# A conditional overflow path moved from the end of each mixture of experts to behind its first four experts, and five modulation chunks moved with it

## The chip, the cores and the metric

The kernel runs on one core of a Trainium2 chip, as one program. The metric is the device time of one execution in microseconds (us); lower is better. Several engines work side by side in a core: TensorE (PE, matrix multiplications; PEld is its loading of weights into the array), VectorE (DVE), ScalarE (ACT), GpSimd (POOL) and SyncE (SP), which here does nothing but issue transfers from the chip's memory (DMAs). Each engine executes its own instructions in order, and waits at semaphores for the others.

## What is computed

Two layers of a backbone over 256 latent tokens and 256 context tokens of width 1024. Each layer has three token mixers on one input projection, and then a mixture of experts. Cut to what matters here:

```python
for l in range(2):
    mod = silu(c) @ w_mod[l] + b_mod[l]          # modulation: 6 vectors of 1024
    h = modulate(rms_norm(x, g_norm[l, 0]), sh1, sc1)
    x = x + gt1 * token_mixers(h, ...)           # starts with h @ w_in[l]
    h = modulate(rms_norm(x, g_norm[l, 1]), sh2, sc2)
    x = x + gt2 * hier_moe(h, ...)               # 32 experts, top 2 for each token
# an expert: (silu(h @ w_gate) * (h @ w_up)) @ w_down, times the router's weight
```

Layer 0 treats all 512 tokens. Layer 1 needs only the latent ones in its experts, 256 tokens.

## The kernel before, in words

`mixers(l)` and `moe(l)` run for l = 0 and then l = 1. A tiling framework puts the instructions of each engine in an order of its own, by estimated due times. It does not move instructions across a conditional block (`tc.If`); between two such blocks it mixes pieces of the program that the code writes one after the other.

**The experts.** `moe` takes the 32 experts in eight groups of four (q = 0 to 7). For each group, `gather` (L1237) picks the tokens of its experts by matrix multiplications with one-hot matrices (`one_hots`, L1226), up to 32 tokens for each expert; `gate_up` (L1274) multiplies them with eight slabs of weights of 1 MB; `swiglu` (L1281 to L1284) works on ACT and DVE; `act_T` (L1294) transposes its result on PE; `down` (L1309) multiplies with four more slabs; and `combine` (L1203 on PE, L1208 on DVE) adds the result to the residual `xT` (tiles called qkv in the traces). `scatter_mats` (L1256, L1259) builds the matrices for `combine`. In layer 0 all this is done for two halves of the tokens (`ns` = 2), in layer 1 for one.

**The slabs.** The weights come through a ring of slots: seven in layer 0; sixteen in layer 1, of which two are used only once. `fetch_up` and `fetch_down` issue the transfers on SP (L1010), in the order of use, and each waits until PE has used up the slab that stood in its slot. In layer 1 the sixteen slabs of q = 0 and q = 1 are fetched ahead of the experts.

**The overflow path.** An expert may be chosen by more than 32 tokens. Then the slots do not do, and a dense path treats the tokens that are left. All of it stands in a block `tc.If(top >= 1024 + CAP)` at the end of `moe`. The highest rank is loaded from memory into a register of each engine (L1359, an instruction TENSOR_LOAD), and each engine branches over the block if there is no overflow (L1361, COMPARE_AND_BRANCH). In the run shown there is none in either layer. The body is 162 rows of PE's order in layer 0 and 103 in layer 1; 125 and 89 on DVE; 30 on SP.

**The layer boundary.** At the end of layer 0's `moe` stand, in the code: the last `combine`; the split of the weights for layer 1's first projection into two parts (`prep`, L221 and L222); five modulation chunks (`mod_chunk`: a fetch of 1 MB at L1355, sixteen multiplications at L238, a copy at L241, two transposes at L243, and L246 and L247 on DVE); the conditional block; the spill of `xT` to memory (L1430). Then `mixers(1)` begins. Its first projection (`pre_w`, L333 to L335: three products for each pair of tiles, 48 in all) works on `xT` times a scale (`scaled`, L369 on ACT and L370 on DVE, sixteen each), before the norm is known. `shift_share` (L399) computes what the shift adds. The norm takes the sums of squares (`Stats`, L276), a column sum on PE (L285), L289 on DVE, a power on POOL (L292), and a broadcast on PE and ACT (L300, L304). Then `shifted` (L322, L327, L329, L378, L379) forms the normalised input h that all further projections use.

## Time and profile before

| | us |
|---|---|
| runs of the kernel before | 1631.34, 1634.6, 1635.05 |
| median | 1634.6 |
| the profiled execution | 1629.37 |
| its span (first to last instruction) | 1627.5 |
| experts of layer 0, from the first gather to the last combine | 709.4 to 970.7 |
| from there to the end of the second projection of layer 1 | 970.7 to 1021.3 |
| experts of layer 1, from the first gather to the last residual | 1407.0 to 1622.4 |

The profile is of one execution. All times below are on its axis; us from the span's start. [...] A line of waits names the instruction that stood, and the one that let it go. "PEq" and "PEldq" are PE's own sequencer, "SPq" is SP's.

### The profile page before, as it was taken

The page shows a single profiled execution, that of the slowest core. Times are in us where ns is not written, and L with a number is a line of the kernel's source. Part 1 is how long each engine was busy: PE and PEld are TensorE (multiplying, and loading weights), DVE is VectorE, ACT ScalarE, POOL GpSimd, SP SyncE. Part 2 cuts the span into 40 slices and gives each one's busy share as a digit, 9 for nine tenths or more (in the row PEclk, how much of TensorE's full clock was granted, in tenths as well). Part 3 has the DMA queues.
Part 4 walks back from the last instruction along what each step waited for, and adds up shares of the span by engine and source line. Part 5 has one row for each costly group of instructions (what it writes and reads, how often), then busy time and mean ns, then how long its engine had stood idle before and what let it go on. Part 6 is the DMA issues. An engine that isn't in the chain of part 4 may idle for free. (4 is left out here: it accounts for less than half of the span.)

```text
span 1627.5 us, 26096 instructions
## 1 busy us (share of the span) xinstructions
PE 1529.6 (94%) x10725; PEld 1058.8 (65%) x10725; DVE 788.3 (48%) x1774; ACT 571.8 (35%) x1125; POOL 183.2 (11%) x162
## 2 busy tenths in 40 slices
PE   5999999999999999989999997999999999897875
PEld 3688789767767778844434435989978789632221
DVE  4637943443345425363333457378456556441222
ACT  4425642443344333131211135356355444211100
POOL 2200320100011003010000003003101112100000
PEclk9999999999999999989999998999999999898888
DMA  8552334323322154349999994542225448699998
GB/s 303 194 172 79 108 107 156 117 76 115 127 98 84 40 179 149 121 166 382 375 398 413 377 409 185 209 142 74 91 104 175 169 148 325 231 411 416 417 418 325
DMA packets 57199, 349.26 MB, mean 215 GB/s; under 512 B 6912, under 2 KB 8032, under 8 KB 20336
## 3 DMA queue, kind: packets, MB, share of 16 engines
q1 hardware_dynamic: 54720, 341.02, 54.9%
q10 hardware_dynamic: 1616, 5.24, 0.9%
q0 software_dynamic: 736, 1.24, 0.4%
q8 instruction: 88, 1.44, 0.4%
q14 instruction: 39, 0.32, 0.1%
HBM read 344.33 MB, written 3.15 MB: 213 GB/s over the span
## 5 line engine op out<-in xcount | busy, mean ns | idle before, releaser
L222 DVE TENSOR_TENSOR wlo<-wraw,whi 128x1024 fp32r<-128x1024 f32 (+1 forms) x152 | 190.6, 1254 | 169.3 <-ACT whi L221 154.2
L333 PE MATMUL mm<-h,whi 128*128 128x512 f32 (+1 forms) x656 | 226.9, 348 | 0.0
L334 PE MATMUL mm<-h,whi 128*128 128x512 f32 (+1 forms) x656 | 223.4, 342 | 0.0
L335 PE MATMUL mm<-h,wlo 128*128 128x512 f32 (+1 forms) x656 | 222.2, 342 | 0.0
L221 ACT CAST whi<-wraw 128x1024 fp32r<-128x1024 f32 (+1 forms) x152 | 155.6, 1026 | 172.3 <-PE mm L334 68.7
L333 PE MATMUL mm<-whi,h 128*128 128x256 f32 (+1 forms) x640 | 183.1, 289 | 0.0
L335 PE MATMUL mm<-whi,h 128*128 128x256 f32 (+1 forms) x640 | 182.9, 288 | 0.0
L334 PE MATMUL mm<-wlo,h 128*128 128x256 f32 (+1 forms) x640 | 182.3, 286 | 0.0
L333 PEld LDWEIGHTS mm<-h,whi 128*128 128x128 f32 x656 | 123.8, 189 | 35.5 <-issue 17.9
L335 PEld LDWEIGHTS mm<-h,wlo 128*128 128x128 f32 x656 | 123.5, 189 | 22.6 <-issue 10.1
L334 PEld LDWEIGHTS mm<-h,whi 128*128 128x128 f32 x656 | 124.2, 190 | 16.9 <-issue 5.3
L333 PEld LDWEIGHTS mm<-whi,h 128*128 128x128 f32 x640 | 121.5, 191 | 6.6 <-issue 4.0
L334 PEld LDWEIGHTS mm<-wlo,h 128*128 128x128 f32 x640 | 122.2, 191 | 1.0 <-DVE G L763 0.5
L335 PEld LDWEIGHTS mm<-whi,h 128*128 128x128 f32 x640 | 121.7, 191 | 1.5 <-issue 1.4
L1274 PE MATMUL at<-qkv,y 128*32 128x512 f32 x792 | 101.2, 606 | 8.0 <-DMA qkv<-in_wgu 8.0
L1208 DVE SCALAR_TENSOR_TENSOR qkv<-mm,c_modT,qkv 128x256 f32<-128x256 f32 x192 | 80.2, 477 | 34.6 <-PE mm L1203 34.6
L618 DVE TENSOR_REDUCE nmx<-at 128x1 f32<-128x512 f32 (+1 forms) x96 | 56.7, 598 | 54.7 <-PE at L604 53.9
L1274 PE MATMUL at<-wraw,y 128*32 128x512 f32 x552 | 73.7, 634 | 7.8 <-DMA wraw<-in_wgu 7.8
L1282 DVE SCALAR_TENSOR_TENSOR a<-a,at 128x256 f32<-128x256 f32 x24 | 10.1, 420 | 141.0 <-ACT a L1281 141.0
L536 POOL TENSOR_TENSOR s1p<-s1p,c_powm 128x8 f32<-128x8 f32 (+1 forms) x24 | 43.3, 1806 | 302.4 <-DVE s1p L534 101.1
L620 ACT ACTIVATE a<-at,nmx 128x512 f32<-128x512 f32 (+1 forms) x96 | 59.3, 619 | 34.3 <-DVE nmx L618 34.1
L1281 ACT ACTIVATE a<-at 128x256 f32<-128x256 f32 x24 | 9.2, 383 | 176.4 <-PE at L1274 171.3
(373 smaller groups left out, 2579.1 us busy)
## 6 DMA issues: line engine op xcount, KB each, us to landing
qkv<-in_wgu SPq DMA_DIRECT2D x62, 1024.0 KB, 11.6
wraw<-in_win SPq DMA_DIRECT2D x56, 1024.0 KB, 4.9
wraw<-in_wgu SPq DMA_DIRECT2D x42, 1024.0 KB, 11.4
wraw<-in_wmod SPq DMA_DIRECT2D x39, 1024.0 KB, 5.0
qkv<-in_wdn SPq DMA_DIRECT2D x31, 1024.0 KB, 9.6
wraw<-in_wdn SPq DMA_DIRECT2D x19, 1024.0 KB, 10.9
h<-in_wgu SPq DMA_DIRECT2D x14, 1024.0 KB, 17.6
wraw<-in_wbr SPq DMA_DIRECT2D x24, 512.0 KB, 3.4
```

What stands on the lines that cost most here:

```text
L221: nc.scalar.copy(hv, src)
L222: nc.vector.tensor_sub(lv, src, hv.bitcast(F32))
L333: nc.tensor.matmul(out_, lhsT=lh, rhs=rh, start=first, stop=False)
L334: nc.tensor.matmul(out_, lhsT=lh, rhs=rl, start=False, stop=False)
L335: nc.tensor.matmul(out_, lhsT=ll, rhs=rh, start=False, stop=last)
L536: nc.gpsimd.tensor_tensor(out=r, in0=v, in1=powm[:, :2 * H], op=ALU.pow)
L618: nc.vector.tensor_reduce(nmx[:, hf:hf + 1], S[hf], axis=AX.X, op=ALU.max, negate=True)
L620: nc.scalar.activation(P[hf], S[hf], AF.Exp, bias=nmx[:, hf:hf + 1], scale=1.0, accum_out=sm[:, hf:hf + 1])
L1208: nc.vector.scalar_tensor_tensor(xT[f][:, c], p[:, c], modT[l][:, 40 + f, v_:v_ + 1], xT[f][:, c], op0=ALU.mult, op1=ALU.add)
L1274: nc.tensor.matmul(gps[v_][CAP * e:CAP * e + CAP], lhsT=xe[v_][:, k, s0:s0 + CAP], rhs=w[e], start=(k == 0), stop=(k == KT - 1))
L1281: nc.scalar.activation(th[:, 0:256], gp[:, 0:256], AF.Tanh, bias=0.0, scale=0.5)
L1282: nc.vector.scalar_tensor_tensor(th[:, 0:256], th[:, 0:256], 1.0, gp[:, 0:256], op0=ALU.add, op1=ALU.mult)
```

## The change

Three things are done.

- **The block moves.** It becomes the function `overflow`, called once in each `moe` after everything that the code writes for q = 0: the first `gate_up`, `swiglu`, the fetches, `scatter_mats(1)`, the gathers and `act_T(0)`. Its body is rewritten to need only small tiles: it loads 512 columns of weights at a time into working tiles (`a2`) and transposes the tokens anew for each expert, since at this place the large slots hold weights that are in use. The body is 662 rows of PE's order in layer 0 and 334 in layer 1; 313 and 169 on DVE; 390 and 198 on SP.
- **The fetches.** `fetch_up` and `fetch_down` put their wishes in a list (`pending`); `pump` issues them as slots come free, and `give_back` returns a slot as soon as a slab is used. The order of the transfers and the number of slots stay.
- **The modulation chunks.** The five chunks leave the end of `moe`. In `mixers(1)`, three are fetched into tiles `y` ahead of the first projection and computed behind it, and two more follow by `mod_fill(2)`.

The diff, cut to its core; the body of the block keeps its arithmetic.

```diff
--- before.py
+++ after.py
@@ -699,9 +699,19 @@
+        held = []
+        if l == 1:
+            for tag in ("y", "y", "y"):
+                m, w = mods.pop(0), s8(tag, [KT, 256])
+                nc.sync.dma_start(w, T["wmod"][m])
+                held.append((m, w))
         for c in range(2):
             if c < len(pre_w):
                 proj_f(pre_w[c], N, lambda i, p: use_k(2 * c + i, p, True), h0, l0)
+                for m, w in held:
+                    mod_chunk(*m, pat, w)
+                mod_fill(2 if held else 0)
+                held = []
...
-            slot_tags[:] = ["qkv"] * 4 + ["mg", "y"] + ["qkv"] + ["h"] * 2 + ["wraw"] * 2 + ["mg", "wraw"] + ["whi", "wlo"] * 3
+            slot_tags[:] = ["qkv"] * 4 + ["mg", "y"] + ["qkv"] + ["h"] * 2 + ["wraw"] * 2 + ["mg", "wraw"] + ["whi"] * 3
...
+    def pump():
+
+        while pending and slot_tags:
+            key, src = pending.pop(0)
+            fetched[key] = fetch_slot(slot_tags.pop(0), src)
+
+    def take(key):
+        return fetched[key][1]
+
+    def give_back(key):
+        tag = fetched.pop(key)[0]
+        if tag not in ("mg", "y"):
+            slot_tags.append(tag)
+        pump()
...
-            fetched.setdefault(("up", q), []).extend(fetch_slot(T["wgu"][l, q, k]) for k in ks)
+            pending.extend((("up", q, k), T["wgu"][l, q, k]) for k in ks)
+            pump()
...
-                w = fetched["up", q][k]
+                w = take(("up", q, k))
...
+                give_back(("up", q, k))
...
+        def overflow():
+
+            top = nc.values_load(mi[0:1, 0:1], min_val=0, max_val=2048,
+                                 skip_runtime_bounds_check_because="the key is 1024 + a rank below 512, or a rank")
+            with tc.If(top >= 1024 + CAP):
...
+                def weights(src):
+                    w = a2([512])
+                    nc.sync.dma_start(w, src.rearrange("o p n -> p (o n)"))
+                    return w
+
+                with tc.For_i(0, NQ, 1) as q4:
+                    one = bass.ds(q4, 1)
+                    for e in range(4):
...
+                        for t in range(ntt):
+                            gp = pat()
+                            for k in range(KT):
+                                q = ptr()
+                                c = slice(128 * k, 128 * k + 128)
+                                for part, ht in enumerate((hth, htl)):
+                                    nc.tensor.matmul(
+                                        q[:, :128], lhsT=ht[t // 2][:, t % 2, c].bitcast(F32), rhs=ident,
+                                        start=(part == 0), stop=(part == 1))
+                                hk = a2([512])[:, :128]
+                                nc.vector.tensor_copy(hk, q[:, :128])
+                                nc.tensor.matmul(
+                                    gp, lhsT=hk, rhs=weights(T["wgu"][l, one, k, :, e]), start=(k == 0), stop=(k == KT - 1))
...
-                aT = act_T(q - 1)
+                if q > 1:
+                    aT = act_T(q - 1)
...
+            if q == 0:
+                aT = act_T(0)
+                overflow()
         down(NQ - 1, act_T(NQ - 1))
         combine(NQ - 1)
         if l == 0:
             lead.append((prep(T["win"][1, 12]), norm_scale(1, 0, slice(0, KT))))
-            for _ in range(5):
-                w = s8("qkv", [KT, 256])
-                nc.sync.dma_start(w, T["wmod"][mods[0]])
-                mod_chunk(*mods.pop(0), pat, w)
-
...
-        top = nc.values_load(mi[0:1, 0:1], min_val=0, max_val=2048,
-                             skip_runtime_bounds_check_because="the key is 1024 + a rank below 512, or a rank")
-        with tc.If(top >= 1024 + CAP):
...
-            if nxt[0] is not None:
-                nxt[0].n = 0
-                for f in range(KT):
-                    nxt[0].step(xT[f])
-            else:
-                for f in range(0, KT, 2):
-                    emit(f)
         return nxt[0]
```

**TensorE in layer 0, around the first four experts.** Before, the last gathers for q = 2 and 3 are followed by the transposes of q = 0 (L1294, `tr`) and by `gate_up` of q = 1 (L1274):

```order
L1237 MATMUL mm_6531<-whi_6452,h_6188 128x256
L1294 MATMUL tr_6541<-c_ident,a_1158_6457 128x128 x2
L1274 MATMUL at_6548<-qkv_6089,y_6293 32x512
L1294 MATMUL tr_6541<-c_ident,a_1159_6461 128x128 x2
L1274 MATMUL at_6548<-qkv_6089,y_6293 32x512 x3
L1274 MATMUL at_6549<-qkv_6089,y_6294 32x512 x4
```

After (gathers are L1260, transposes L1318, `gate_up` L1297):

```order
L1260 MATMUL mm_6497<-whi_6442,h_6162 128x256
L1318 MATMUL tr_6507<-c_ident,a_1153_6447 128x128 x2
L1318 MATMUL tr_6507<-c_ident,a_1154_6451 128x128 x2
L1279 MATMUL ao_8593<-rwT_6146,t_1850_8590 128x512
L1342 TENSOR_LOAD mi_6152
L1344 COMPARE_AND_BRANCH
...
L1344 UNCONDITIONAL_BRANCH
L1297 MATMUL at_8390<-qkv_6340,y_6267 32x512 x4
L1297 MATMUL at_8391<-qkv_6340,y_6268 32x512 x4
```

The transposes now stand together, and between them and the next `gate_up` stand the load, the branch and the body of the block.

**TensorE at the layer boundary.** Before: the last combine, the first of the five chunks, the block, then L285, `shift_share`, and the first projection with the norm's broadcast (L300) in it:

```order
L1203 MATMUL mm_8353<-wlo_8039,mg_8239 128x256 x2
L238 MATMUL at_8378<-qkv_8376,c_cpad 32x256 x8
L243 MATMUL at_8378<-c_ident,t_1475_8387 128x128 x2
...
L1359 TENSOR_LOAD mi_6178
L1361 COMPARE_AND_BRANCH
...
L285 MATMUL ao_9171<-c_ones,acc_8284 128x1 x4
L399 MATMUL at_9187<-whi_8365,spad_9130 32x256
...
L333 MATMUL mm_9284<-qkv_9132,whi_8365 128x512
L333 MATMUL mm_9285<-qkv_9132,whi_8365 128x512
L300 MATMUL ao_9180<-c_ident,s1p_9177 128x128 x4
```

After (combine is L1226; `mm_10417` is the first projection's sum, `mm_10575` the second's):

```order
L1226 MATMUL mm_10209<-wlo_9897,mg_10114 128x256
L399 MATMUL at_10314<-whi_10241,spad_10257 32x256
L238 MATMUL at_10486<-y_10411,c_cpad 32x256 x8
...
L333 MATMUL mm_10417<-qkv_10259,whi_10241 128x512
...
L333 MATMUL mm_10417<-qkv_10260,whi_10245 128x512
L285 MATMUL ao_10298<-c_ones,acc_10160 128x1 x4
...
L238 MATMUL mm_10471<-wraw_10469,c_cpad 32x256 x7
L238 MATMUL at_10501<-y_10413,c_cpad 32x256 x8
L238 MATMUL mm_10533<-wraw_10531,c_cpad 32x256 x3
L300 MATMUL ao_10307<-c_ident,s1p_10304 128x128 x4
L238 MATMUL mm_10550<-wraw_10548,c_cpad 32x256 x8
L333 MATMUL mm_10575<-h_10336,whi_10567 128x512
```

The projection follows the combine with no block between them. L285 stands near its end, and the broadcast L300 behind two modulation chunks and a part of a third.

**VectorE at the same place.** Before: the norm's L289, the scaled input, then L322 to L379 for h:

```order
L289 TENSOR_SCALAR s1p_9176<-ao_9171 128x4
L370 SCALAR_TENSOR_TENSOR qkv_9134<-qkv_5610,smp_8373,qkv_9132 128x256 x8
L370 SCALAR_TENSOR_TENSOR qkv_9135<-qkv_5611,smp_8373,qkv_9133 128x256 x8
L322 TENSOR_TENSOR a_1656_9214<-qkv_5610,acc_9185 128x512
...
L329 TENSOR_SCALAR t_1655_9213<-a_1656_9214,smp_8373,c_modT_129 128x256
...
L222 TENSOR_TENSOR wlo_9356<-wraw_9353,whi_9355 128x1024
...
L322 TENSOR_TENSOR a_1668_9256<-qkv_5611,acc_9185 128x512
L379 TENSOR_TENSOR h_9211<-t_1655_9213,h_9209 128x512
```

After:

```order
L276 TENSOR_TENSOR acc_10160<-acc_10160,a_2119_10236 128x512
L407 TENSOR_REDUCE shb_10258<-at_10314 128x4
L289 TENSOR_SCALAR s1p_10303<-ao_10298 128x4
L322 TENSOR_TENSOR a_2144_10341<-qkv_5610,acc_10312 128x512
...
L699 SCALAR_TENSOR_TENSOR qkv_10409<-mm_10417,acc_10312 128x512
...
L329 TENSOR_SCALAR t_2143_10340<-a_2144_10341,smp_10249,c_modT_129 128x256
...
L722 TENSOR_SCALAR qkv_10409<-qkv_10409,shb_10258 128x256 x2
L222 TENSOR_TENSOR wlo_10568<-wraw_10565,whi_10567 128x1024
...
L322 TENSOR_TENSOR a_2156_10383<-qkv_5611,acc_10312 128x512
L379 TENSOR_TENSOR h_10338<-t_2143_10340,h_10336 128x512
```

The scaled input has left this stretch (it stands among the combine's additions). Between L322 and the first L379 stand now work on the first projection's results (L699, L722) and more weight splits (L222).

**SyncE in layer 1.** Before: the last two slabs of `down` for q = 0, then those of `gate_up` for q = 2:

```order
L1010 DMA qkv_13622<-in_wdn 128x2048
L1010 DMA qkv_13859<-in_wgu 128x2048
L1010 DMA h_13861<-in_wgu 128x2048
L1010 DMA h_13863<-in_wgu 128x2048
L1010 DMA wraw_13865<-in_wgu 128x2048
```

After:

```order
L1016 DMA qkv_15026<-in_wdn 128x2048
L1016 DMA qkv_15071<-in_wgu 128x2048
L1016 DMA h_15073<-in_wgu 128x2048
L1342 TENSOR_LOAD mi_14899
L1344 COMPARE_AND_BRANCH
...
L1344 UNCONDITIONAL_BRANCH
L1016 DMA h_16080<-in_wgu 128x2048
L1016 DMA wraw_16086<-in_wgu 128x2048
```

Six slabs (four of `down`, two of `gate_up`) stand ahead of the block, and the others behind it.

## Rows read from the trace of the kernel before

**Rows 1.** Windows: us, busy PE, PEld, DVE, ACT, POOL; clock, DMA share, GB/s.
```profile
800.00:900.00 100.00, 98.15 (x808) 44.03 (x801) 40.00 (x96) 18.12 (x33) 0.00 (x0) 1.00 0.99 407
```

**Rows 2.** Waits of 711 to 960 us: who for whom; us, times, longest.
```profile
PE tr L1294 <- DVE a L1284: 3.1, 5, 0.6
```

**Rows 3.** Windows of the layer boundary.
```profile
970.66:981.92 11.26, 7.26 (x90) 3.02 (x90) 8.76 (x22) 4.25 (x9) 2.55 (x2) 1.00 0.47 183
981.92:985.62 3.70, 0.00 (x0) 0.03 (x1) 0.34 (x2) 0.92 (x3) 0.00 (x0) 0.96 0.45 179
985.62:995.61 9.99, 6.83 (x40) 3.56 (x41) 6.59 (x17) 5.57 (x14) 1.03 (x1) 0.50 1.01 383
995.61:1008.89 13.28, 13.28 (x75) 10.41 (x74) 11.00 (x14) 8.86 (x15) 9.33 (x4) 1.00 0.15 62
1008.89:1021.29 12.40, 12.40 (x71) 9.53 (x67) 10.01 (x20) 6.55 (x11) 2.97 (x9) 1.00 0.60 211
```

**Rows 4.** Window of layer 1's mixture of experts.
```profile
1500.00:1600.00 100.00, 74.54 (x409) 20.22 (x401) 19.81 (x45) 8.50 (x17) 0.00 (x0) 0.85 1.02 417
```

**Rows 5.** Lines L1359, L1361: ns min/median/max, first, last start; who waited.
```profile
L1359 PEldq TENSOR_LOAD <-mi x2: 320/404/489, 981.5 to 1620.3; - x2
...
L1361 PEldq COMPARE_BRANCH  x2: 3382/3532/3681, 982.1 to 1620.7; - x2
L1361 DVEq COMPARE_BRANCH  x2: 63/68/72, 982.7 to 1621.6; - x2
...
  PE ao L285: 3.7, 1
```

**Rows 6.** Waits of 966 to 1021 us.
```profile
PEld at L399 <- issue: 5.6, 8, 4.0
```

**Rows 7.** Timeline of SP's queue at the end.
```profile
1617.73 5.61 SPq L1216 DMA_DIRECT2D out_x<-qkv  x4
```

**Rows 8.** Timeline of TensorE after the first four experts of layer 0.
```profile
741.04 1.05 PE L1274 MATMUL at<-qkv,y 128*32 128x512 f32 x2
742.01 0.44 PE L1294 MATMUL tr<-c_ident,a 128*128 128x128 f32 x2
```

**Rows 9.** Windows where TensorE's clock comes back.
```profile
1406.00:1407.00 1.00, 1.00 (x7) 0.89 (x6) 1.00 (x6) 0.26 (x1) 0.00 (x0) 0.50 0.00 0
...
1409.00:1410.00 1.00, 1.00 (x10) 1.00 (x9) 0.96 (x3) 0.62 (x2) 0.00 (x0) 1.00 0.00 0
```

**Rows 10.** Timeline of VectorE at the boundary: start us, us, work.
```profile
975.01 0.86 DVE L1208 SCALAR_TENSOR_TENSOR qkv<-mm,c_modT,qkv 128x256 f32<-128x256 f32 x2
...
987.90 6.42 DVE L370 SCALAR_TENSOR_TENSOR qkv<-qkv,smp,qkv 128x256 fp32r<-128x256 f32 x16 [0.24 <-DVE s1p L289]
997.89 2.40 DVE L322 TENSOR_TENSOR a<-qkv,acc 128x512 f32<-128x512 f32 x2 [3.57 <-ACT acc L304]
...
1004.51 0.68 DVE L379 TENSOR_TENSOR h<-t,h 128x512 fp32r<-128x512 f32 x1
...
1015.09 1.28 DVE L379 TENSOR_TENSOR h<-t,h 128x512 fp32r<-128x512 f32 x2
```

**Rows 11.** Timeline of TensorE at the boundary.
```profile
1007.89 1.07 PE L238 MATMUL mm<-wraw,c_cpad 128*32 128x256 f32 x16
...
1021.29 0.39 PE L333 MATMUL mm<-h,whi 128*128 128x256 f32 x1
```

**Rows 12.** Timeline of TensorE at the same place.
```profile
1406.99 3.90 PE L1237 MATMUL mm<-S,h 128*128 128x256 f32 x24
...
1425.20 0.62 PE L1274 MATMUL at<-h,y 128*32 128x512 f32 x1
```

**Rows 13.** Timeline of SP's queue at the start of layer 1's experts.
```profile
1411.94 6.08 SPq L1010 DMA_DIRECT2D qkv<-in_wdn  x4
...
1423.75 2.86 SPq L1010 DMA_DIRECT2D h<-in_wgu  x2
```

**Rows 14.** Page part 6: line engine op xcount, KB each, median us to landing.
```profile
wraw<-in_win SPq DMA_DIRECT2D x56, 1024.0 KB, 4.9
```

More of the change, by code (lines that the diff above doesn't have):

```diff
@@ L982, in tile_backbone @@
     NQ = E_NUM // 4
+    pending = []
     def start_fetch(l, nt):
@@ L993, in start_fetch, with fetch_slot @@
             fetch_down(l, 0)
-    def fetch_slot(src):
-        def slot(k):
-            tag = slot_tags.pop(0)
-            if tag not in ("mg", "y"):
-                slot_tags.append(tag)
-            if tag not in ("wraw", "whi", "wlo"):
-                return s8(tag, [k, 512])
-            t = wp.tile([128, k * 512], F32R if tag != "wraw" else F32, tag=tag, name=nm(tag), bufs=WB)
-            return (t.bitcast(F32) if tag != "wraw" else t).rearrange("p (a b) -> p a b", b=512)
-        h = 2 if slot_tags[0] in ("whi", "wlo") else 1
-        w = Slabs([slot(4 // h) for _ in range(h)], 4 // h)
+    def fetch_slot(tag, src):
+        w = Slabs([
+            s8(tag, [4, 512]) if tag in SB else wp.tile(
+                [128, 2048], F32, tag=tag, name=nm(tag), bufs=WB).rearrange("p (a b) -> p a b", b=512)], 4
+        ) if tag != "whi" else Slabs([
+            wp.tile([128, 1024], F32R, tag=t, name=nm(t), bufs=3).bitcast(F32).rearrange("p (a b) -> p a b", b=512)
+            for t in ("whi", "wlo")], 2)
         for i, t in enumerate(w.tiles):
             nc.sync.dma_start(t, src[:, w.per * i:w.per * i + w.per])
-        return w
+        return tag, w
+    def pump():
[9 more added lines that the diff above has]
+        pump()
     def fetch_up(l, q, ks=range(KT)):
         if q < NQ:
-            fetched.setdefault(("up", q), []).extend(fetch_slot(T["wgu"][l, q, k]) for k in ks)
+            pending.extend((("up", q, k), T["wgu"][l, q, k]) for k in ks)
+            pump()
     def fetch_down(l, q):
         if q < NQ:
-            fetched["down", q] = [[fetch_slot(T["wdn"][l, q, cc, kk]) for kk in range(2)] for cc in range(2)]
+            pending.extend((("down", q, cc, kk), T["wdn"][l, q, cc, kk]) for cc in range(2) for kk in range(2))
+            pump()
     class Router:
@@ L1299, in down @@
         def down(q, aT):
-            wd = fetched.pop(("down", q))
             for v_ in range(ns):
@@ L1304, in down @@
                 c = slice(512 * cc, 512 * cc + 512)
+                wd = [take(("down", q, cc, kk)) for kk in range(2)]
                 for v_ in range(ns):
```

93 lines of the change are left out of this document (38 added, 55 removed).

## The prediction

> **What bounds the kernel now.** I read the windows first, stage by stage, since the three places that the change touches have different limits. In layer 0's experts TensorE stands still for almost nothing: it is busy in 98.15 of 100 us [rows 1], and the largest idle time of its matrix multiplications there is 3.1 us in five pieces, for VectorE [rows 2]. The transfers run at 407 GB/s beside it. So this stage is bound by TensorE, and what stops TensorE there is paid in full. At the layer boundary TensorE is far from full: from 970.66 to 1021.29, 50.6 us, it is busy for 39.8, and 6.8 of these at clock 0.50 [rows 3]. In layer 1's experts TensorE is busy for 75 of 100 us while the transfers run at 417 GB/s and take a share of 1.02 [rows 4]. This stage is bound by transfers: a slab of 1 MB takes 2.5 us at that rate, and each us in which no transfer runs is paid at the end.
>
> The block itself is seen at two places. At the boundary TensorE's load of the register takes 0.3 to 0.5 us and its branch 3.38 to 3.68, while VectorE's branch takes 0.07, and the column sum L285 waits 3.7 us for TensorE's sequencer [rows 5]. Soon after, `shift_share` stands for another 4.0 us for which no wait is shown [rows 6]. The branch at the program's end lies beside the output's transfers, whose issue lasts from 1617.73 to 1623.34 [rows 7].
>
> **Layer 0's experts: the block arrives.** Before, the two pairs of transposes of q = 0 stand 0.97 us apart with the first multiplications of q = 1 between them [rows 8]. After, nothing of q = 1 may go ahead of the branch, so TensorE waits there for VectorE; I take 0.5 (0 to 1.0). The load adds 0.4. For the branch the trace has 3.38 and 3.68 on the same engine and 0.07 on VectorE [rows 5]. The jump is now over 662 rows of order and was over 162 and 103; if the 0.3 between the two came from these 59 rows, 662 rows would give 6.2 (an estimate from these rows). I take 3.5, the same engine's, with 0.07 and 6.2 as ends. After the gap at the boundary the clock is 0.50 for 10 us, with the second hole in them [rows 3]. At the start of layer 1's gathers, with no such hole, it is 0.50 in 1406 to 1407 and 1.00 in 1409 to 1410, with TensorE busy in both [rows 9]. I take 3 us at half speed, so 1.5 lost (0 to 5). All slots are full at this place, so the transfers can't use the gap. Sum: 0.5 + 0.4 + 3.5 + 1.5 = 5.9 (0.5 to 12). A gain is excluded, as no work leaves this stage. SP, VectorE and ScalarE branch too, over bodies up to 390 rows. If theirs took 3.5 us, it would lie beside TensorE's; what they have next (the slab for q = 2, the split for `down`) is not wanted until TensorE has done `gate_up` of q = 1.
>
> [...]
>
> **The layer boundary: the block and the chunks leave.** What can be won at most: 39.8 us of work, with 6.8 of them at half speed, would take 36.4 at full clock; 50.6 - 36.4 = 14.2. But what will set the end there? I follow the new order.
>
> VectorE: before, the combine's last addition ends at 975.87 [rows 10]. In the new order sixteen L370 (6.4 us) and three more L276 (0.7 each, 2.0) stand among the additions, and the last L351 come later as ScalarE has L369 ahead of L350: the last L276 ends near 985 (975.9 + 6.4 + 2.0 + 0.7). TensorE: the projection needs the weight splits and `shift_share`, so it starts near 978 rather than at 995.61. Its 48 products took 12.3 us (995.61 to 1007.89) [rows 3, 11]; it ends near 990. L285 stands near its end, at 988.5; then come L289, and L300 behind two and a half chunks (1.07 each [rows 11]): 993. The broadcast is there at 993.5, against 997.89 before [rows 10]. So of the 17 us that the projection starts earlier, 4.4 are left.
>
> VectorE then goes from the broadcast to the first L379. Before, that took 6.6 us (997.89 to 1004.51 [rows 10]). Now two L699, four L722 and one more L222 stand ahead of it, and all four L322: with the durations of the trace 3.7 + 2.6 (L329) + 1.3 + 1.1 + 2.4 = 11.1, so the first L379 starts at 1004.6, and the last ends near 1013.4 (1016.4 before). The second projection's first half needs them all: it ends at 1014. Its second half takes 5.6, and in the new order two chunks' L238 (2 x 1.07) and three or more L243 pairs (0.44 each) stand in it. So the next projection begins at 1014 + 5.6 + 2.1 + 1.3 = 1023, against 1021.29 [rows 11]. That is +1.9; TensorE has stood for some 13 us before, so a part of the second projection may run at half speed, and I take +2.5. The same number of chunks is done by then in both orders (seven). Ends: -14.2, and +7 if all of the projection's first half runs late. Two of the moved fetches stand ahead of the last two slabs of `down` on SP and delay them by 2.5 or 5 us; the slabs were ahead of their use, and I count 0 (to 3 if they were not).
>
> **Layer 1's experts.** Before, 24 gathers take 3.9 us ahead of the first `gate_up` [rows 12]; now it is 32, so the first slot is free 1.2 us later. Six slabs can be issued ahead of the block. Before, the first was issued at 1411.94 [rows 13], so now at 1413.1; data flow some 1.6 us later, from 1414.7, and six slabs of 2.5 us last until 1429.7. Before, the seventh followed the sixth within 2.9 us [rows 13]. Now the next slab needs a slot that `gate_up` of q = 1 gives back. TensorE reaches the block at about 1425, as before it reached this `gate_up` at 1425.20 [rows 12]; with 0.4 + 3.5 for load and branch, and 1 to 2 for the first slab at half speed, the slot is free near 1430.5. A slab that is fetched alone lands 4.9 us after its issue [rows 14], of which 2.5 are its data at the full rate; so data flow again 2 us or so after the issue, near 1432.5. The hole is 2.8 us, the stage loses 1.2 + 2.8 = 4.0 (1 to 8), and since it is bound by transfers all of it reaches the end.
>
> **The rest.** The block at the program's end costs nothing now; -0.5 for what it may hold up (-1.5 to 0). `pump` keeps order and slots: 0. The dropped statements in the body aren't executed.
>
> **Sum.** 5.9 + 2.5 + 4.0 - 0.5 = +11.9 on the profiled execution's 1629.4, so 1641.3. That execution lies 5.2 us (0.32%) below the median of the runs shown; on the median 1634.6 it gives 1646.5. I give that. A measurement of this kernel can tell about 0.3% from no change, 4.9 us; below 1629.7 is faster, above 1639.5 slower.
>
> **The rivals.** *The branch is cheap where it now stands* (TensorE's branch takes VectorE's 0.07, as its code is at hand or the sequencer is ahead). Then no clock is lost: layer 0 pays 1.0, layer 1 1.7, and 1.0 + 2.5 + 1.7 - 0.5 = +4.7: 1639.3, no difference that can be told. For it: VectorE's rows. Against: both of TensorE's.
> *The boundary gives all that it can.* Place: 970.66 to 1021.29; price: -14.2 instead of +2.5, so 5.9 - 14.2 + 4.0 - 0.5 = -4.8: 1629.8, not slower, and faster if any other term is below my value. It decides in its favour from the point where the second projection ends 9.4 us earlier than before (5.9 + 4.0 - 0.5), at 1011.9. That asks for the broadcast near 981. For it: the idle time is there. Against: the new order's place of L300 and VectorE's load.
> *A second hole behind each block*, as the 4.0 us at L399 [rows 6]: +4.0 in each stage, so +19.9: 1654.5. For it: that hole follows a branch within 7 us. Against: there small instructions follow, and here long ones.
> That the change does not do what it says is excluded by the order: block, chunks and projection stand where the words put them.
>
> [...]
>
> **How the numbers follow.** My forecast 0.48 (own range 1640 to 1653), the cheap branch 0.17, the full gain at the boundary 0.20, the second hole 0.15. Faster: half of the full gain and 0.10 from low ends of the others, 0.20. No difference: most of the cheap branch, the rest of the full gain and a little of the forecast, 0.25. Slower: 0.55. The range goes from the full gain's 1629 to just beyond the second hole, 1656.
>
> **What would show it.** Layer 0: TensorE idle for 4 to 5 us near 743 to 747, then clock 0.50 for about 3 us; if the branch takes 0.07 the first rival holds. Boundary: the first projection starting near 978, the broadcast near 993 to 994, TensorE idle for over 10 us, the first L379 near 1004 to 1006 (all plus layer 0's shift). Layer 1: a hole of 2 to 4 us in the transfers near 1430. I am wrong if the second projection follows the first without an idle stretch, or if the hole in the transfers is missing.

## The result and the profile after

The changed kernel takes 1645.5 us (median, 1644.75 to 1646.45) against 1633.0 for the kernel before beside it: a ratio of 1.0079, interval 1.0059 to 1.0099, so slower by 10 to 16 us. The forecast was 1646.5 and "slower". The profiled execution of after takes 1644.75 us (span 1643.0), that of before 1629.4 (span 1627.5).

I cut both traces at the same six events: the end of the first layer's first `gate_up`, the end of that layer's last `down` on its first half of columns, the start of the projection behind the second one, the second layer's first gather, the end of its last residual, and the end of the span. The differences between after and before, in us, add up to the 15.5 between the spans:

| stretch | before | after | difference | predicted |
|---|---|---|---|---|
| up to the first `gate_up`'s end | 735.8 | 735.2 | -0.6 | 0 |
| layer 0's experts | 228.1 | 234.3 | +6.2 | +5.9 |
| layer boundary | 57.4 | 59.9 | +2.5 | +2.5 |
| layer 1's mixers | 385.7 | 385.2 | -0.6 | 0 |
| layer 1's experts | 215.4 | 224.9 | **+9.5** | **+4.0** |
| end | 5.1 | 3.6 | -1.5 | -0.5 |

Two terms came as forecast, and one is more than twice its size. The block's rows, by line, engine and operation (min/median/max in ns, first and last start), answer to [rows 5]; the smaller value of TensorE's branch is layer 0's, the larger layer 1's:

```profile
L1344 PEldq COMPARE_BRANCH  x2: 3887/5043/6199, 741.3 to 1432.4; - x2
...
L1344 DVEq COMPARE_BRANCH  x2: 68/70/72, 741.8 to 1431.9; - x2
L1344 DVEq EVENT_SEMAPHORE  x2: 21/21/21, 745.2 to 1437.9; - x2
L1344 PEldq EVENT_SEMAPHORE  x2: 51/51/51, 745.3 to 1438.7; - x2
```

TensorE's branch takes 3.9 us in layer 0 and 6.2 in layer 1. VectorE's branch is recorded with 0.07, but its next instruction follows 3.4 us later in layer 0 and 6.0 us later in layer 1: VectorE waits too, and the 0.07 didn't show it. TensorE's timeline behind the two blocks (start, us, work, idle before and who ended it):

```profile
745.52 5.19 PE L1297 MATMUL at<-qkv,y 128*32 128x512 f32 x24 [4.34 <-DVE smp L313]
```
```profile
1432.01 0.38 PE L1282 MATMUL ao<-rwT,t 64*128 64x256 f32 x1
1438.94 1.92 PE L1297 MATMUL at<-h,y 128*32 128x512 f32 x4 [6.54 <-PEq L1344]
1441.68 1.07 PE L1297 MATMUL at<-h,y 128*32 128x512 f32 x2 [0.82 <-issue]
```

In layer 1 a second hole stands behind the first: after four multiplications TensorE is idle for 0.82 us with no wait shown. The windows of 2 us over the same place (busy time of each engine; TensorE's clock as a share of its full one; DMA share, GB/s) answer to [rows 4]:

```profile
1434.00:1436.00 2.00, 0.00 (x0) 0.00 (x0) 0.00 (x0) 0.00 (x0) 0.00 (x0) 0.50 1.07 426
1436.00:1438.00 2.00, 0.00 (x0) 0.00 (x0) 0.00 (x0) 0.00 (x0) 0.00 (x0) 0.50 0.54 180
1438.00:1440.00 2.00, 1.06 (x4) 0.22 (x5) 0.57 (x3) 0.00 (x0) 0.00 (x0) 0.50 0.11 41
1440.00:1442.00 2.00, 1.18 (x7) 0.20 (x7) 0.00 (x0) 0.00 (x0) 0.00 (x0) 0.50 0.00 0
1442.00:1444.00 2.00, 2.00 (x12) 0.48 (x8) 0.00 (x0) 0.00 (x0) 0.00 (x0) 0.50 0.03 8
1444.00:1446.00 2.00, 2.00 (x16) 0.57 (x12) 0.00 (x0) 0.00 (x0) 0.00 (x0) 0.50 0.55 147
```

The last two columns are what to read: in a stage that the transfers bound, they run dry from 1437 to 1445. The missing share adds up to 7.5 us (0.92 + 1.78 + 2.00 + 1.94 + 0.90). What they wait for stands in SyncE's queue, in the row of the sixth and the seventh slab:

```profile
1428.16 15.81 SPq L1016 DMA_DIRECT2D h<-in_wgu  x2
```

Before, these two were issued within 2.86 us [rows 13], now within 15.81. The seventh is issued at 1443.63, when the eighth multiplication with the first slab of q = 1 has ended (1443.61): it waits for TensorE to give back that slot, and not for SyncE's own jump. Before, the same stretch had no hole:

```profile
1440.00:1442.00 2.00, 2.00 (x15) 0.56 (x9) 0.21 (x1) 0.00 (x0) 0.00 (x0) 1.00 1.02 408
```

Who ends the wait can be seen in the DMA queues. Queue q8 carries instructions in packets of 16 KB (88 packets, 1.44 MB in all). One of them follows each of TensorE's branches over a long body, so I take q8 for TensorE's; the other engines' branches are followed by packets of 8 KB on q14. From layer 1's branch at 1432.4 up to 1436.0 the weight queue q1 is full and q8 moves nothing; then, in 1436.00 to 1436.25, its packet comes, and TensorE goes on 2.7 us later (queue, kind: packets, MB, share):

```profile
q1 hardware_dynamic: 201, 1.51, 103.4%
```
```profile
q1 hardware_dynamic: 11, 0.09, 86.1%
q8 instruction: 1, 0.02, 27.7%
```

At the boundary, the windows answer to [rows 3]: the first projection (983.56 to 996.50), a stretch of chunks and waiting, TensorE nearly idle for 6.2 us, and the second projection, the start of it at half clock:

```profile
983.56:996.50 12.94, 12.94 (x60) 10.05 (x60) 8.55 (x19) 5.24 (x13) 2.25 (x2) 1.00 0.32 130
996.50:1006.53 10.03, 6.43 (x72) 3.11 (x71) 5.86 (x9) 5.23 (x9) 4.87 (x4) 0.82 0.58 209
1006.53:1012.75 6.22, 0.80 (x2) 0.29 (x2) 6.22 (x10) 2.67 (x5) 1.26 (x1) 0.50 0.55 179
1012.75:1029.34 16.59, 16.57 (x91) 11.91 (x92) 8.91 (x20) 9.16 (x18) 2.90 (x9) 0.88 0.31 113
```

### The profile page after: what moved, and what is told of

It is laid out like the page before. It is cut to its first block, busy times and chain, and to the rows that moved or that the text cites. A ratio compares the mean times of both kernels' runs of the same rounds, so it can differ in the third digit from the quotient of the medians.

```text
span 1643.0 us, 26108 instructions
## 1 busy us (share of the span) xinstructions
PE 1531.9 (93%) x10725; PEld 1059.3 (64%) x10725; DVE 790.6 (48%) x1774; ACT 571.5 (35%) x1125; POOL 182.6 (11%) x162
## 3 DMA queue, kind: packets, MB, share of 16 engines
q8 instruction: 88, 1.44, 0.3%
## 5 line engine op out<-in xcount | busy, mean ns | idle before, releaser
L222 DVE TENSOR_TENSOR wlo<-wraw,whi 128x1024 fp32r<-128x1024 f32 (+1 forms) x152 | 191.5, 1260 | 164.7 <-ACT whi L221 148.7
L1297 PE MATMUL at<-qkv,y 128*32 128x512 f32 x792 | 102.5, 622 | 17.8 <-DMA qkv<-in_wgu 13.4
L1231 DVE SCALAR_TENSOR_TENSOR qkv<-mm,c_modT,qkv 128x256 f32<-128x256 f32 x192 | 80.1, 477 | 35.8 <-PE mm L1226 35.8
L1297 PE MATMUL at<-wraw,y 128*32 128x512 f32 x552 | 74.3, 646 | 5.5 <-DMA wraw<-in_wgu 5.5
## 6 DMA issues: line engine op xcount, KB each, us to landing
wraw<-in_wdn SPq DMA_DIRECT2D x19, 1024.0 KB, 10.8
```

Source lines behind the costliest of these rows:

```text
L222: nc.vector.tensor_sub(lv, src, hv.bitcast(F32))
L1231: nc.vector.scalar_tensor_tensor(xT[f][:, c], p[:, c], modT[l][:, 40 + f, v_:v_ + 1], xT[f][:, c], op0=ALU.mult, op1=ALU.add)
L1297: nc.tensor.matmul(gps[v_][CAP * e:CAP * e + CAP], lhsT=xe[v_][:, k, s0:s0 + CAP], rhs=w[e], start=(k == 0), stop=(k == KT - 1))
```

## The experiments

A ratio is that to the kernel before on the same chip. "Stage" means a stretch of the table above, cut in the same way in each trace; the same stage varies by 1 to 2 us between the seven kernels without a dear branch in it: 228.1 to 229.1 us for layer 0's experts, 213.9 to 216.1 for layer 1's.

**Each block alone, and none.** The call of the block is left out, or put under a condition on the layer:

```diff
-                overflow()
+                if l == 0:
+                    overflow()
```

(`l == 1` for the third.)

> The changed kernel with the conditional block taken out of both layers (the overflow path is left out of the computation). My theory: each stage gives back what its trace shows, 5.9 us in moe 0 and 9.5 us in moe 1, and the 2.7 us at the boundary stay, so 1630 us (1628 to 1633) against 1645.5 for the changed kernel. Rival: part of what the block costs is slack that something else takes (the first down projection waits for swiglu and its DMAs anyway), and then only the branches themselves come back, 3.8 + 6.1 us less what the holes hide: 1636 to 1639 us.

> The changed kernel with the block in layer 0 alone (layer 1's overflow path is left out). My theory: moe 1 gives back its 9.5 us, so 1636 us (1634 to 1639). Rival, that moe 1 lost the time to its fetch order and not to the block: 1642 to 1646 us.

> The changed kernel with the block in layer 1 alone (layer 0's overflow path is left out). My theory: moe 0 gives back its 5.9 us, so 1639.6 us (1637.5 to 1642), with layer 1's branch still at some 6 us. Rival, that the branch in layer 1 is dear because layer 0's has pushed the instruction fetch about: its branch falls to 3.9 us and the time to 1636 or 1637 us.

| kernel | us | ratio and interval | layer 0's experts | boundary | layer 1's experts | end |
|---|---|---|---|---|---|---|
| no block | 1630.8 | 1.0013 (0.9999 to 1.0027) | 228.6 | 60.9 | 215.8 | 3.4 |
| layer 0 only | 1637.4 | 1.0037 (1.0022 to 1.0052) | 234.5 | 59.8 | 215.1 | 3.6 |
| layer 1 only | 1638.1 | 1.0047 (1.0030 to 1.0063) | 228.6 | 60.0 | 221.8 | 3.4 |

All three times lie where the first theory put them. But the kernel before takes 1629.4 us beside these runs and 1633.0 beside the first, so the ratios are the surer measure. By them (1.0079 and 1.0013) the change is 10.8 us (some 7 to 15) faster without its two blocks; the theory has 15.4 and the rival of the first run 6.5 to 9.5, and the whole time doesn't tell them apart. The stages do: without the block layer 0's experts are 5.7 us shorter and layer 1's 9.1, so more comes back than the branches alone. On this one chip layer 0's block costs 6.6 us by the medians (1637.4 - 1630.8) and 5.9 by its stage, layer 1's 7.2 and 6.0. What is left of the change without any block is 2 us (0 to 4) slower than before with its block. Between "layer 1 only" and the changed kernel nothing differs in layer 1 but the place of its code in the program. The rival there fails in its mechanism, as the branch still takes 6.06 us; but the stage is 3.1 us shorter, since the second hole is absent. TensorE's timeline of that kernel behind the block:

```profile
1432.93 1.94 PE L1297 MATMUL at<-h,y 128*32 128x512 f32 x8 [6.59 <-PEq L1344]
1434.61 3.37 PE L1297 MATMUL at<-wraw,y 128*32 128x512 f32 x16
```

**The chunks alone.** The block stays at its old place, without the small buffers:

> The kernel before with nothing but the five modulation chunks moved behind the second layer's first projection; the block stays behind the last expert. My theory: the chunks cost at their new place what they save at the old one, give or take the boundary's branch that is still there, so 1630 to 1637 us around 1633. Rival, that the chunk move is a gain of its own and the block's place eats it: the 14 us or so of chunk work leave the path and the time falls to 1622 to 1628 us. Third reading, that the chunks moved are a loss of their own and the block's removal from the boundary hid it: 1638 us or more.

1631.3 us, ratio 1.0007 (0.9994 to 1.0020): no difference that can be told. The boundary takes 58.0 us; VectorE's splits of the next input (L370) stand behind the block there, from 986.38 on. The move of the chunks alone is neither the gain nor the loss.

**What the old block cost at the boundary.** The kernel before without its block:

```diff
-        top = nc.values_load(mi[0:1, 0:1], ...
-        with tc.If(top >= 1024 + CAP):
-            ...
```

> The kernel before with its conditional block taken out of both layers (the overflow path is left out). Theory A, the block at the boundary was free or better: it also stood as a fence, so that vector work of the second layer could not get ahead of the last residuals; without it the stage from the last experts to the second layer's projections takes as long or up to 3.5 us longer than the 57.4 us of before, the end gives back 1.5 us, and the time is within 3 us of before. Theory B, the 3.7 us branch and the 3.2 us hole behind it stood on the path: they come back, with the 1.5 us at the end, and the time is 5 to 8 us under before.

1623.8 us, ratio 0.9952 (0.9933 to 0.9971): 8 us faster than before. Theory A, mine, falls, and B holds: the boundary takes 53.2 us instead of 57.4, and the end 3.4 instead of 5.1. So the change did take 4.2 us out of the boundary, and yet its boundary is longer. Without any block the same stage takes 53.2 with the chunks at their old place and 60.9 with the chunks moved. With the old block in its place the move of the chunks cost nothing that could be told, so the 7.8 us point at the order that the two moves leave behind together.

**What the order costs.** VectorE's timeline of after shows it; L1231 are the last experts' residuals, L370 the splits of the next layer's input, L276 the statistics:

```profile
971.77 0.48 DVE L370 SCALAR_TENSOR_TENSOR qkv<-qkv,smp,qkv 128x256 fp32r<-128x256 f32 x1
972.17 0.87 DVE L1231 SCALAR_TENSOR_TENSOR qkv<-mm,c_modT,qkv 128x256 f32<-128x256 f32 x2
972.95 2.69 DVE L370 SCALAR_TENSOR_TENSOR qkv<-qkv,smp,qkv 128x256 fp32r<-128x256 f32 x4
...
980.82 1.90 DVE L370 SCALAR_TENSOR_TENSOR qkv<-qkv,smp,qkv 128x256 fp32r<-128x256 f32 x2
982.63 3.22 DVE L1231 SCALAR_TENSOR_TENSOR qkv<-mm,c_modT,qkv 128x256 f32<-128x256 f32 x8
```

Eight of the sixteen splits stand ahead of the last residuals (the expectation below says nine). The last residual ends 16.4 us into the stage (985.85), against 12.0 before [rows 10] and 12.0 in before without its block. The next experiment takes that order away, in the kernel without a block, by one small instruction that makes the splits' scale `A` depend on the last residual:

```diff
+            A = norm_scale(1, 0, slice(0, KT))
+            nc.vector.scalar_tensor_tensor(
+                A, xT[KT - 1][:, 256:256 + 2 * KT].rearrange("p (a b) -> p a b", b=2), 0.0, A, op0=ALU.mult, op1=ALU.add)
-            lead.append((prep(T["win"][1, 12]), norm_scale(1, 0, slice(0, KT))))
+            lead.append((prep(T["win"][1, 12]), A))
```

> The changed kernel without its block (the overflow path is left out), and with one VectorE instruction of 128x16 that makes the second layer's input scale depend on the last residual of the first, so that the sixteen L370 splits can't stand ahead of it. Theory A, the boundary's 2.5 us come from VectorE doing nine of these splits ahead of the residuals, 0.4 us each: the last residual comes some 3.6 us earlier, the 60.9 us that the stage took without the block fall by 2 to 4 us, and the time is 2 to 4 us under that without the fence. Theory B, the first projection then starts as much later as the statistics come earlier: the stage takes 60 to 63 us and the time stays or grows by up to 2 us.

1624.5 us, ratio 0.9960 (0.9946 to 0.9974), by the ratios 8.6 us under the same kernel without that instruction (1.0013, on another chip). VectorE now ends the residuals before the first split:

```profile
978.58 3.21 DVE L1231 SCALAR_TENSOR_TENSOR qkv<-mm,c_modT,qkv 128x256 f32<-128x256 f32 x8
...
982.40 0.16 DVE L1445 SCALAR_TENSOR_TENSOR smp<-qkv,smp 128x16 f32<-128x16 f32 x1
983.13 1.36 DVE L370 SCALAR_TENSOR_TENSOR qkv<-qkv,smp,qkv 128x256 fp32r<-128x256 f32 x2 [0.58 <-ACT qkv L369]
```

The last residual ends 13.6 us into the stage, and the stage takes 55.8 us instead of 60.9. Theory A holds, with 5.1 us where it had 2 to 4; the whole time fell by more than that too, and layer 1's experts, which the edit doesn't touch, are 1.9 us of it (213.9 for 215.8). So of the 7.8 us, 5.1 are this order; what the other 2.7 are stays open.

**What a branch costs: a short body against the long one.** The block's body is cut to one or two instructions for each engine, at the same two places of the code:

```diff
             with tc.If(top >= 1024 + CAP):
                 nc.vector.tensor_scalar(over, key, float(1024 + CAP), None, op0=ALU.is_ge)
                 nc.vector.tensor_tensor(out=dw[:, :ntt], in0=dw[:, :ntt], in1=over, op=ALU.mult)
-                ...
-                with tc.For_i(0, NQ, 1) as q4:
-                    ...
+                w = a2([512])
+                nc.sync.dma_start(w, T["wgu"][l, 0:1, 0, :, 0].rearrange("o p n -> p (o n)"))
+                q = ptr()
+                nc.tensor.transpose(q[:, 0:128], w[:, 0:128], ident)
+                hk = a2([512])[:, :128]
+                nc.scalar.copy(hk, q[:, :128])
```

> The changed kernel with the same two blocks at the same two places, but a body of a handful of instructions, one to three for each engine (the work of the overflow path is left out). Theory A, the price of a block is the fetch of instructions behind a far jump: the target now lies in what has been fetched, the branches fall from 3.9 and 6.2 us to under 1 us each on TensorE, the halved clock and the second hole go too, and the time is that of the kernel with no block at all plus at most 3 us, so 1630 to 1634 us. Theory B, the price is that of the register load, the compare and the refill whatever the distance: branches of 3 us and more stay in both layers and the time is 1640 to 1646 us.

1632.0 us, ratio 1.0003 (0.9994 to 1.0013). Theory A holds: TensorE's branch is 0.2 us in both layers, and layer 1's experts take 215.6 us, as with no block.

```profile
L1344 PEldq COMPARE_BRANCH  x2: 206/220/235, 747.5 to 1436.7; - x2
```

In TensorE's order the place did not stay the same. The block now stands within `gate_up` of q = 1; in layer 0 TensorE still works on multiplications from ahead of it when the branch is done, and hardly stops:

```profile
745.79 4.49 PE L1297 MATMUL at<-qkv,y 128*32 128x512 f32 x38
750.46 1.06 PE L1297 MATMUL at<-qkv,y 128*32 128x512 f32 x8 [0.17 <-PEq L1344]
```

Such work could hide a fetch, so the short idle time alone would prove nothing. But there is none to hide: q8 shows no packet for 12.1 us behind the first branch and for 8.9 behind the second, where over the long body one starts within 0.8 to 4.5 us.

So load, compare and branch are cheap here: 0.3 and 0.5 us for TensorE's load in the changed kernel, 0.2 for its branch over the short body. Over the long one the branch takes 3.9 and 6.2 us, and a packet of instructions comes behind it. From this pair I take the price for that of fetching the code that the jump leads to; that is my reading, as no view shows which code a packet holds.

**Why layer 1's branch is dearer.** Three attempts. The first two hold back the expert slabs behind a flag until the block is passed, from the first group's `gate_up` on, or from the stage's start:

```diff
+            hold.append(1)
...
-        while pending and slot_tags:
+        while pending and slot_tags and not hold:
...
                 overflow()
+                hold.clear()
+                pump()
```

> The changed kernel, whose transfers of expert weights in the second layer are held back from the middle of the first group of experts until behind the block, so that the weight queue is empty when the branch falls. Theory A, the instruction packet waits behind the weight transfers: it comes within 1.2 us of the branch and the branch takes 3.7 to 4.0 us as in the first layer instead of 6.2. Theory B, the second layer's branch is dear for another reason (its place in the program): it stays at 6 us. The time itself says little, since the transfers held back come later: 1640 to 1655 us.

> The changed kernel, with the second layer's expert transfers held back from the stage's very start: only the first group's eight weight tiles are fetched ahead, all others wait until behind the block, so that the weight queue is empty for several us when the branch falls. Theory A, the instruction packet waits behind weight transfers: it comes within 1.2 us of the branch, and TensorE's branch takes 3.4 to 4.0 us as in the first layer. Theory B, the place in the program makes the branch dear: it stays at 6 us. The whole time is no evidence: the second group then waits some 20 us for its weights, 1655 to 1675 us.

Neither could tell anything as meant: the scheduler put the held transfers ahead of the block again, and the weight queue was full when the branch fell. In both traces SyncE issues the same six slabs ahead of its branch as in the changed kernel, though the code issues them behind the block. So the words above, that the framework moves nothing across a conditional block, don't hold for these transfers, nor for the multiplications ahead of the short body. The branches took 6.0 and 7.0 us, and the packet came 3.5 and 4.5 us behind the branch. That is no evidence for theory B, as nothing had been made quiet. The times are of one execution each: 1644.9 us, and 1649.8, below the 1655 to 1675 expected, as the second group did not wait for its weights.

The third attempt takes the transfers away: in layer 1 the second group uses the first group's weights, so no slot comes free ahead of the block.

```diff
-            fetch_up(l, 1)
...
-                w = take(("up", q, k))
+                key = ("up", 0 if l == 1 and q == 1 else q, k)
+                w = take(key)
...
-                give_back(("up", q, k))
+                if l == 0 or q > 0:
+                    give_back(key)
```

> The changed kernel, whose second layer uses the first group's weights for the second group too and does not fetch the second group's own (that group's result is left out). So its slots are given back only behind the block, and no weight transfer is issued in the 20 us ahead of the branch. Theory A, the instruction packet waits behind weight transfers: it comes within 1.2 us of the branch, and TensorE's branch takes 3.4 to 4.0 us as in the first layer, instead of 6.2. Theory B, the place in the program makes the branch dear: it stays at 6 us. The whole time is no evidence, since a fifteenth of the layer's weights is not fetched.

(It is 8 of 96 slabs that aren't fetched, a twelfth and not a fifteenth.) From 1420 up to the packet no weight transfer runs. The branch's rows, the queues in 1434.50 to 1434.75, and TensorE behind the block:

```profile
L1345 PEldq COMPARE_BRANCH  x2: 3699/3913/4127, 742.1 to 1433.5; - x2
```
```profile
q8 instruction: 1, 0.02, 31.8%
```
```profile
1437.55 1.92 PE L1297 MATMUL at<-qkv,y 128*32 128x512 f32 x4 [4.05 <-PEq L1345]
1440.54 5.17 PE L1297 MATMUL at<-qkv,y 128*32 128x512 f32 x26 [1.07 <-issue]
```

Layer 1's branch, the shorter of the two (layer 0's next instruction, at 746.3, is 4.2 us behind its branch), takes 3.7 us instead of 6.2. The packet comes 1.0 us behind the branch instead of 3.6. Theory A holds. The second hole stays, 1.07 us here, so it is not due to traffic.

The opposite test moves layer 0's block from behind the first group to behind the fourth, into the midst of transfers:

```diff
+        at = 3 if l == 0 else 0
...
-            if q == 0:
-                aT = act_T(0)
+            if q == at:
+                aT = act_T(q)
                 overflow()
```

> The changed kernel with the first layer's block moved from behind the first group of experts to behind the fourth, where the weight transfers run at some 420 GB/s without a break; the second layer's block stays. Theory A, the packet waits behind the transfers: the first layer's branch, 3.9 us before, grows to 5 to 7 us. Theory B, it has nothing to do with the transfers: 3.9 us stay. Time 1643 to 1650 us.

```profile
L1344 PEldq COMPARE_BRANCH  x2: 4858/5635/6412, 842.2 to 1439.2; - x2
```

Layer 0's branch grows from 3.9 to 4.9 us, just under theory A's 5 to 7; the one execution takes 1651.2 us, just over the 1643 to 1650 expected. The weight queue was full at first, but the packet came at 844.5 as that queue ran low: SyncE stood before the block too, as shown by its branch at 835.8, and what it had issued was running out. TensorE's branches in these kernels, with the first quarter of a microsecond in which q8 shows a packet behind the branch:

| kernel, place | branch at | packet | from branch to packet | weight queue until then | TensorE goes on at |
|---|---|---|---|---|---|
| before, boundary | 982.1 | 983.0 | 0.9 | empty | 985.5 |
| no transfers, layer 1 | 1433.5 | 1434.5 | 1.0 | empty | 1437.3 |
| looped body, layer 0 | 741.8 | 742.75 | 1.0 | full, then ends | 745.5 |
| after, layer 0 | 741.3 | 742.5 | 1.2 | full, then ends | 745.3 |
| block in traffic, layer 0 | 842.2 | 844.5 | 2.3 | 95%, then ends | 847.2 |
| looped body, layer 1 | 1429.3 | 1432.5 | 3.2 | full, then ends | 1435.4 |
| layer 1 only, layer 1 | 1426.6 | 1430.0 | 3.4 | full | 1432.7 |
| held from the first group, layer 1 | 1433.3 | 1436.75 | 3.5 | full | 1439.3 |
| after, layer 1 | 1432.4 | 1436.0 | 3.6 | full | 1438.7 |
| block in traffic, layer 1 | 1439.2 | 1442.75 | 3.6 | full | 1445.6 |
| held from the start, layer 1 | 1437.5 | 1442.0 | 4.5 | full, then ends | 1444.6 |

From packet to the next instruction it is 2.5 to 2.9 us in each row. What varies is the wait for the packet: 0.9 to 1.2 us where the weight queue is empty, or ends soon behind the branch, and 3.2 to 4.5 where it stays full for so long. TensorE's seven other branches over a long body in these runs (the end of before, both of the chunks alone, layer 0's in four kernels) are all of the first kind, with 0.8 to 1.4 us to the packet and 2.5 to 3.1 from there.

**A complete kernel made better.** The changed kernel with the small instruction of the fenced one, and a loop over the four experts of a group in the block's body:

```diff
-                    for e in range(4):
+                    with tc.For_i(0, 4, 1) as e4:
+                        ex = bass.ds(e4, 1)
...
```

> The changed kernel, complete, with two edits: the 128x16 instruction that keeps the second layer's splits behind the last residuals, and a loop over the four experts of a group in place of four copies in the block's body, which cuts the body to a quarter (some 170 TensorE rows in the first layer, 90 in the second, from 660 and 330). By the runs so far the first edit gives 5 or 6 us at the boundary. Theory A, any jump past more than a handful of rows is fetched anew, as the kernel before shows with a body of 160 rows and 3.7 us: branches as before, 1637 to 1641 us. Theory B, a body of 90 rows is near enough: the second layer's branch falls under 1 us and gives back 6 to 9 us too, 1629 to 1633 us; if both are near, 1625 to 1628 us.

1638.1 us, ratio 1.0042 (1.0026 to 1.0058): some 6 us better than the changed kernel, and still slower than before. The boundary takes 55.1 us. TensorE's branches stay, as theory A says, at 3.6 and 5.9 us over 170 and 90 rows; VectorE's jump over its shorter body became cheap (its next instruction follows 0.6 us after the branch, where it was 3.4):

```profile
L1344 PEldq COMPARE_BRANCH  x2: 3647/4763/5879, 741.8 to 1429.3; - x2
...
L1344 DVEq COMPARE_BRANCH  x2: 63/68/72, 742.3 to 1428.8; - x2
L1344 DVEq EVENT_SEMAPHORE  x2: 21/21/21, 742.9 to 1429.3; - x2
```

Of the complete kernels none was faster than before. How short TensorE's body would have to be, between a handful of rows and 90, stays open.

## Why the prediction came out

**The whole.** 1645.5 against 1646.5, but not each step. The terms sum to +11.9; the profiled pair shows +15.5, and the medians +12.6. So the time fits better than the terms do: the sum was added to a median of 1634.6 from three runs of before, 1.6 us above the 1633.0 of the comparison, and layer 1's experts were 5.5 us short. That the total lies within 1 us is luck; that it is slower, by an amount of this size and for these causes, is not.

**Layer 0's experts: right.** +6.2 for +5.9. TensorE's gap is 4.34 us; load and branch had 3.9 there and the wait for VectorE 0.5. That wait is absent: the transposes run at 740.12 without a stop. The clock is at 0.50 from 745.5 to about 750.5; that loses 2.5 us where I had 1.5. Against the kernels without a block the stage is 5.7 us longer. The choice of 3.5 over the 6.2 that grows with the length of the jump was right: over 662 rows the branch takes 3.9, and over the 170 of the looped body 3.6. In before, too, the longer branch is not the one over the longer body: the boundary's, at 982.1 over 162 rows, takes 3.38, and the end's, at 1620.7 over 103, takes 3.68.

**The boundary: right in size and in its steps.** All places are to be read 5.6 us later, for the two differences ahead of them (+6.2 - 0.6). The first projection starts at 983.6, so 978 as forecast. The last L276 ends at 991.9, so 986.3 for 985. The broadcast is there at 1000.6, so 995 for 993.5. The first L379 starts at 1012.0, so 1006.4 for 1004.6, and the next projection at 1029.3, so 1023.7 for 1023. TensorE waits 5.42 us in one piece for L379; with the shorter pauses it stands still for 9.0 us between the two projections (996.50 to 1012.75), a little under the 10 that was named as a sign. What I had not separated are the parts behind the +2.5: the old block's going gives 4.2 (1623.8 us run), and the new order takes more, 5.1 of it by splits ahead of residuals (the fenced run). The prediction saw these L370 among the additions and charged them to the statistics; it didn't ask what the stage would be without them.

**Layer 1's experts: the step that failed.** The term was 4.0, 1.2 for the later first slot and 2.8 for a hole in the transfers, and 9.5 was measured, beyond its bound of 8. The 1.2 is right: the first slab of `down` is issued at 1420.38 instead of 1411.94, 8.4 us later, 0.9 more than the first gather. The hole is 7.5 us instead of 2.8, and 0.9 + 7.5 is 8.4 of the 9.5. In the "layer 1 only" kernel the share missing from 1430 to 1438 is 4.7, and 0.9 + 4.7 is 5.6 of 6.4. The hole was mis-sized as I took the branch of the quiet boundary, 3.5, for a place where the transfers run at a share of 1.0. There the packet waits 3.6 us instead of the 1.0 of the run without transfers, which makes the branch 6.2 instead of 3.7. The second hole and the half clock then keep TensorE from giving the slot back until 1443.6. The forecast of 1430.5 is 1438.0 with the 7.5 us by which the stage starts later, so the slot came 5.6 us late: 2.7 of that are the branch (6.2 for 3.5). From its first multiplication to the slot TensorE needs 4.7 us here, and 2.0 in "layer 1 only", with the same clock of 0.50 and no second hole; so the second hole is worth 2.7 too. Both had been named: the second hole as a rival of +4.0 for each block, and it came, in layer 1 alone.

**The end: -1.5 for -0.5.** At the far end of its range; before without its block shows the same gain, 5.1 to 3.4.

**The rivals.** The cheap branch was excluded by 3.9 and 6.2 us; VectorE's 0.07, on which it stood, is a record and not the price there, as VectorE stood for 3.4 and 6.0 us behind it. The full gain at the boundary had the idle time on its side, and the run of 1623.8 us shows that 4.2 us were there to be had; the broadcast at 995 instead of the 981 it asked for shows why it didn't come. The second hole was named from [rows 6]; TensorE's row behind it in before is

```profile
992.48 0.68 PE L399 MATMUL at<-whi,spad 128*32 128x256 f32 x4 [3.16 <-issue]
```

There too q8 shows a packet shortly ahead, at 990.03, 2.4 us before TensorE goes on. So it is of the kind that came in layer 1.

## What to carry to other kernels

In these runs a branch over a body of 90 to 662 rows cost TensorE 3.4 to 7.0 us, and 0.2 over a handful of instructions. It cost 3.4 to 3.9 in the rows of the table above where the weight queue was empty or ended within 1.2 us, and 5.9 to 7.0 in those where the packet came 3.2 to 4.5 us late behind a full queue. So place it where the engine would be idle and the queues are quiet, or make the body short; 90 rows were not short enough. A duration taken from one stage holds in another only if what it depends on is the same there: ask what the price is made of before you carry it over. When a block leaves a place, look at what the scheduler now lets pass there: here VectorE work for the next layer stood ahead of the residuals that everything waited for, and one 128x16 instruction gave back 5 us.

## What the chip showed that I had not expected

- The instruction packet comes later where the weights flow: 0.8 to 1.4 us from branch to packet where the weight queue is quiet or soon runs dry, 3.2 to 4.5 where it stays full, and 2.5 to 3.1 from packet to the next instruction in both. One pair of kernels takes the transfers alone away (3.6 against 1.0 us); the other rows agree with it.
- A second packet may follow. In after q8 shows one at 1439.25, and TensorE, idle since 1440.86, goes on at 1441.68, 2.4 us later; with no transfers it is 1437.75 and 1440.54, 2.8 us. The two kernels with held transfers and the one with the block in traffic show such a hole too, of 0.84 to 1.07 us, in layer 1. In "layer 1 only" the packet of 1433.25 stops nothing. The same code with another place in the program behaves differently; the cause is not shown, as no run moved the code alone.
- An engine's branch can read 0.07 us while the engine stands for 3.4 us behind it (VectorE at 741.8 to 745.2): look at the next instruction, not at the branch.
